# The expert stage of a mixer, cross-attention and mixture-of-experts layer on one core: row gathers recorded two experts ahead, apart from their transposes

## The chip, the core and the metric

The kernel runs on one core of one Trainium2 chip. The core has five engines with an instruction queue each: TensorE (PE; its weight loads are listed apart as PEld), VectorE (DVE), ScalarE (ACT), GpSimd (POOL) and SyncE (SP), which here issues transfers and reads registers. Data moves by 16 DMA engines. The metric is the device time of one execution in microseconds (us), lower is better.

## What is computed

The reference is one layer of a streaming encoder: a mixer of attention and gated linear attention, a cross-attention, and a mixture of experts. The change touches the last. Each of 2048 tokens of 1024 channels goes to two of 32 experts, and an expert is a gated pair of projections to 512 channels and one back:

```python
def _hier_moe(h, norm_g, w_group, b_group, w_expert, b_expert, w_gate, w_up, w_down):
    xf = _rmsnorm(h, norm_g).reshape(t, d)
    ...                                             # g_sel, top_i, gate: group, two experts in it, their weights
    flat_id = (g_sel[:, None] * EXPERTS_PER_GROUP + top_i).reshape(-1).astype(jnp.int32)
    ...                                             # tokens sorted by expert into x_pad
    def expert_block(args):
        xb, e = args
        hid = jax.nn.silu(xb @ w_gate[e]) * (xb @ w_up[e])
        return hid @ w_down[e]
    ...
    out = out_pad[dest] * flat_gate[order][:, None].astype(out_pad.dtype)
    y = jnp.zeros((t, d), out.dtype).at[token_of].add(out)
```

## The kernel before

**Number format.** Values in 32 bits are carried as two 16-bit halves, so each product is three matmuls. The weights of an expert, 6 MB, come in 12 loads of 512 KB (`est`, line 1499, issued by SP, pool E of 8 buffers). Each is split into its halves `ew` by one ACT instruction and then one DVE instruction, into pool W of 28 buffers: the 24 of two experts, and 4 for tokens.

**The order.** All instructions are first recorded. A list scheduler then fixes one order for each engine, from the order of recording and some shifts, by a model of durations. Buffers of a pool open in the order of recording, and an engine works strictly in its order. So a wait at the head of an engine's queue holds all that is behind it.

**The expert stage** (`stage_moe`, line 1444) goes through 32 places, which this text numbers 0 to 31: place 0 holds late tokens of expert 0, place 1 is expert 1, and from place 2 on experts come ranked by their number of tokens (`rank`, line 1372, leaves that order in the tensor `order`). `expert_weights` reads a ranked expert's number into a register of SP (the rows `TENSOR_LOAD order`, line 1478). A place has room for 104 to 224 tokens, in blocks of up to 128. A second part of the 128-row places, as the 32 rows of place 20, is its second block.

**One block** goes through these steps: SP loads its list of row numbers and gates (`lt`, line 1533, 6 buffers); POOL gathers the rows of the normed activations, 4 KB a row in two halves of 16 bits, with an indirect DMA (`ex<-xnS,lt`, line 1536, pool Q of 4 buffers); PE transposes them in 16 pieces (`pxT`, pool mm of 3 PSUM banks, 8 pieces to a bank); ACT copies the first bank and DVE the second to `exT` (pool W). Then `expert` (line 1552) does the gate and up products (`pgu`), `sil` and `hid`, and the down product (`py`, in the same 3 banks). ACT scales the result to `ey`, and POOL adds it to the output with an indirect DMA (`out_dram<-ey`, line 1603, here called the scatter). A list buffer is free when its block's scatter has landed, since that reads it; blocks of 64 rows or fewer copy the row numbers to `dst` for their scatter.

**How far ahead.** In the recording, `prepare(n + 1)` stands in front of `expert(n)`: the list, the gather and the transposes of a place are all recorded one place ahead, behind its weights.

Of the kernel before, what the change touches and what calls it, by code (L numbers as in the profile page):

```python
# [8 lines left out]
F16 = mybir.dt.float16  # L9
# [21 lines left out]
NG, NE, DE = 4, 32, 512  # L31
LIST = S + 256
FRONT = -3000
# [5 lines left out]
THR = 0  # L39
CHAIN = 1  # L40
# [4 lines left out]
STAG = "W"  # L45
FIXED = 2
LATE = 2
# [6 lines left out]
CAPS = [224, 190, 182, 172, 168, 160, 160, 154, 152, 150, 148, 146, 144, 142, 138, 136, 132, 128, 128, 126,  # L54
        124, 122, 118, 118, 116, 114, 112, 112, 106, 104, 160, 176, 32]


TAGS = {"W": (4096, 28), "E": (4096, 8), "P": (4096, 3), "X": (4096, 4), "Q": (4096, 4), "t2": (2048, 4), "t1": (1024, 2), "r": (160, 5), "lt": (32, 6),
        "s8": (32, 5), "sq": (32, 6), "mx": (32, 8), "cb": (32, 6), "so": (32, 6), "c8": (32, 5), "c9": (32, 6), "q8": (32, 4), "grT": (512, 1)}
BANKS = {"mm": 3, "av": 1, "sc": 4}  # L60
AP = bass.AP
# [39 lines left out]
class Program:  # L101
# [15 lines left out]
    def tile(self, pool, shape, dtype, name, tag, bufs):  # L117
        t = pool.tile(shape, dtype, name=name, tag=tag, bufs=bufs)
        self.tags[t.tensor.name] = tag
        self.bufs[tag] = bufs  # L120
        return t
# [266 lines left out]
class Layer:  # L388
# [10 lines left out]
    def tile(self, tag, name, shape, dtype, parts=128):  # L399
        assert parts * 0 + mybir.dt.size(dtype) * math.prod(shape) <= TAGS[tag][0], (name, tag)  # L400
        return self.prog.tile(self.sb, [parts] + shape, dtype, name, tag, TAGS[tag][1])

# [1028 lines left out]
    def begin_moe(self):  # L1431

        nc = self.nc
        self.ident16 = self.gate_b[:, 128:192].bitcast(F16)
        nc.vector.tensor_copy(self.ident16, self.ident)
        which, need, self.first = self.expert_weights(None, 0)
        self.prog.shift = EARLY
        cap = CAPS[NE - FIXED]
        tokens = self.tokens(cap, which, need, blocks=LATE)
        self.second = self.expert_weights(None, 1, [self.last] if THR else [], CHAIN)  # L1440
        self.expert(cap, self.first, tokens)
        self.prog.shift = 0

    def stage_moe(self):

        slots = [NE] + [NE - FIXED + e for e in range(1, FIXED)]
        n = (NE - FIXED) // 3
        slots += [k + j * n for k in range(n) for j in range(3)]
        ready = {}

        def prepare(n):
            s = slots[n]
            if n == 0:
                which, need, w = lambda: NE, (), self.first
            elif n < FIXED:
                which, need, w = self.second
            else:
                if n == FIXED:
                    self.rank()
                which, need, w = self.expert_weights(s, None)  # L1460
            self.prog.shift = FRONT
            ready[n] = w, self.tokens(CAPS[s], which, need)
            self.prog.shift = 0
        prepare(0)
        for n, s in enumerate(slots):
            if n + 1 < len(slots):
                prepare(n + 1)
            self.prog.shift = -3000
            self.expert(CAPS[s], *ready.pop(n))
            self.prog.shift = 0  # L1470

    def expert_weights(self, rank, e, after=(), chain=0):

        nc, a, prog = self.nc, self.a, self.prog
        reg = []
        need = []
        if e is None:
            need = [prog.call("sync", lambda nc: reg.append(nc.sync.value_load(
                self.order[0:1, rank:rank + 1], min_val=0, max_val=NE - 1)), [], [self.order], method="value_load")]
        which = (lambda: reg[0]) if e is None else (lambda: e)  # L1480
        return which, need, self.split_expert(which, need + list(after), STAG if e == 0 else "E", chain)

    def split_expert(self, which, need, tag="E", chain=0):
        self.prog.group = "ew"
# [19 lines left out]
            return lambda half, i: tiles[i // k][:, half, i % k]  # L1504
        return get("w_e_gate", D, DE, 2), get("w_e_up", D, DE, 2), get("w_e_down", DE, D, 1)

    def tokens(self, cap, which, need, first=None, blocks=0):

        self.prog.group = "tk"
        nc, prog = self.nc, self.prog  # L1510
        xT = [self.tile("W", "exT", [8, cap], F16) for _ in range(2)]
        rest = []
        for t0 in range(0, cap, 128):
            n = min(128, cap - t0)
            lt = self.tile("lt", "lt", [2], I32)

            parts = 4 if n <= 32 else 2 if n <= 64 else 1

            g = -(-n // 16) * 16
            m = g if parts == 1 else 128 // parts  # L1520
            rest.append((t0, m, lt, parts))

            def load(nc, lt=lt, m=m, t0=t0, parts=parts):
                e = which()
                if first is not None:
                    src = self.lists[bass.ds(first(), m)]
                elif isinstance(e, int):
                    src = self.lists[e * LIST + t0:e * LIST + t0 + m]
                else:
                    src = self.lists[bass.ds(e * LIST + t0, m)]  # L1530
                if parts > 1:
                    src = src[None].to_broadcast([parts, m, 2])
                return nc.sync.dma_start(lt[:m * parts], src)
            prog.call("sync", load, [lt[:m * parts]], [self.lists], need)
            x = self.tile("Q", "ex", [2, D], F16)
            prog.call("gpsimd", lambda nc, x=x, lt=lt, g=g: nc.gpsimd.indirect_dma_start(
                out=x[:g].rearrange("p t d -> p (t d)"), out_offset=None, in_=self.xnS[:S + OFF - blocks * 128],
                in_offset=bass.IndirectOffsetOnAxis(ap=lt[:g, 0:1], axis=0)), [x[:g]],
                      [lt[:g], self.xnS[:S + OFF - blocks * 128]])
            for h in range(2):  # L1540
                p = self.prog.tile(self.ps, [128, 8, 128], F16, "pxT", "mm", BANKS["mm"])
                for k in range(8):

                    d = slice(k // 2 * 256 + k % 2, (k // 2 + 1) * 256, 2)
                    nc.tensor.transpose(p[:, k, :n], x[:n, h, d], self.ident16[:n, :n])
                if h:
                    nc.vector.tensor_copy(xT[h][:, :, t0:t0 + n], p[:, :, :n])
                else:
                    nc.scalar.copy(out=xT[h][:, :, t0:t0 + n], in_=p[:, :, :n])
        return xT, rest  # L1550

    def expert(self, cap, weights, tokens):
        self.prog.group = "ex"
        nc, prog = self.nc, self.prog
# [53 lines left out]
    def stage_over(self):  # L1608
        nc = self.tc.nc
        self.prog.direct = True  # L1610
        count = self.cp.tile([1, 1], F32, name="count")
        nc.vector.memset(count, 0.0)
        total = nc.values_load(self.total[0:1, 0:1], min_val=0, max_val=64)  # L1613
        with self.tc.For_i(0, total, 1):
            sel = self.tile("r", "sel", [NL], F32, 1)
            t = self.tile("r", "ot", [NL], F32, 1)
            f = self.tile("r", "of", [2], F32, 1)
            at = self.tile("r", "oi", [2], I32, 1)
            before, upto, ids, place = (self.over[:, n] for n in range(4))

            nc.vector.tensor_scalar(sel, before, count, None, op0=OP.is_le)
            nc.vector.tensor_scalar(t, upto, count, None, op0=OP.is_gt)
            nc.vector.tensor_tensor(out=sel, in0=sel, in1=t, op=OP.mult)
            nc.vector.tensor_tensor(out=t, in0=sel, in1=ids, op=OP.mult)
            nc.vector.tensor_reduce(out=f[:, 0:1], in_=t, op=OP.add, axis=AX.X)
            nc.vector.tensor_scalar(t, before, count, -128.0, op0=OP.subtract, op1=OP.mult)
            nc.vector.tensor_tensor(out=t, in0=t, in1=place, op=OP.add)
            nc.vector.tensor_tensor(out=t, in0=sel, in1=t, op=OP.mult)
            nc.vector.tensor_reduce(out=f[:, 1:2], in_=t, op=OP.add, axis=AX.X)
            nc.vector.tensor_copy(at, f)  # L1630
            nc.vector.tensor_scalar(count, count, 1.0, None, op0=OP.add)
            e = nc.sync.value_load(at[0:1, 0:1], min_val=0, max_val=NE - 1)
            row = nc.sync.value_load(at[0:1, 1:2], min_val=0, max_val=NL * LIST - 128)
            which = lambda: e
            w = self.split_expert(which, ())
            self.expert(128, w, self.tokens(128, which, (), lambda: row))


# [24 lines left out]
```

## Time and profile before

| | |
|---|---|
| median of 3 runs | 2382.82 us (2374.73 to 2393.74) |
| profiled execution, device time | 2377.83 us |
| its span, first to last instruction | 2376.1 us |
| mean granted TensorE clock | 0.967 |
| PE busy over the span | 2137.9 us (90%) |
| DVE, ACT, POOL busy | 1559.7 (66%), 1339.2 (56%), 750.6 (32%) us |
| expert weight loads | 384 of 512 KB |

The expert stage begins at about 1660 us of the span and lasts to its end. The page cuts the span into 40 slices of about 59 us. Their lines for PE's busy tenths, the granted clock, the busy tenths of the DMA engines and the traffic are:

```profile
PE   6999999999888889889998999994899999888888
PEclk9999999999989999999999999997899999999999
DMA  9544246663357686888785556495989999999995
GB/s 258 155 114 116 81 142 178 192 191 103 111 116 149 145 179 151 184 169 201 168 211 131 116 143 126 117 250 140 300 303 329 345 369 331 325 338 340 358 346 152
```

The expert stage is the last 12 or so of them, with traffic of 300 to 369 GB/s, but for the last slice, against 81 to 258 before. In a row of the trace, a number in brackets is how long the engine was idle before that row, and the arrow names what ended it.

### The profile page before, as it was taken

To read this page: it belongs to the slowest core of one execution; us is meant where nothing else is said; L and a number is where in the kernel's file an instruction comes from. 1 tells how busy PE (TensorE), PEld (TensorE's weight loads), DVE (VectorE), ACT (ScalarE), POOL (GpSimd) and SP (SyncE) were. 2 spreads that over 40 slices of the span, in tenths; PEclk is the share of its full clock that TensorE was granted. 3 is DMA by queue.
4 is the path that set the end of the run, shared out by engine and by line. 5 is a ranking of instruction groups with operands and counts; after the bars stand their busy time and mean duration, and the time that the engine had idled before them with its cause. 6 is when DMAs were issued, how large, how long until landed. Compare 5 with 4: busy or idle time off the path is not lost. (4 is left out here: it accounts for less than half of the span.)

```text
span 2376.1 us, 55935 instructions
## 1 busy us (share of the span) xinstructions
PE 2137.9 (90%) x22153; PEld 1466.6 (62%) x22153; DVE 1559.7 (66%) x3434; ACT 1339.2 (56%) x2848; POOL 750.6 (32%) x622
## 2 busy tenths in 40 slices
PE   6999999999888889889998999994899999888888
PEld 3456646556444445445665777843777887777666
DVE  7454445655588888888534655476666877777774
ACT  6455345554466666665433333444566777667775
POOL 1444235552134444444221222213132322222111
PEclk9999999999989999999999999997899999999999
DMA  9544246663357686888785556495989999999995
GB/s 258 155 114 116 81 142 178 192 191 103 111 116 149 145 179 151 184 169 201 168 211 131 116 143 126 117 250 140 300 303 329 345 369 331 325 338 340 358 346 152
DMA packets 504232, 485.34 MB, mean 204 GB/s; under 512 B 391364, under 2 KB 401886, under 8 KB 503966
## 3 DMA queue, kind: packets, MB, share of 16 engines
q1 hardware_dynamic: 489950, 442.11, 64.9%
q0 software_dynamic: 14016, 39.63, 7.2%
q8 instruction: 175, 2.87, 0.5%
q14 instruction: 91, 0.75, 0.1%
HBM read 306.28 MB, written 83.61 MB: 164 GB/s over the span
## 5 line engine op out<-in xcount | busy, mean ns | idle before, releaser
L166 DVE SCALAR_TENSOR_TENSOR ew<-est,ew 128x1024 f16<-128x1024 f32 x384 | 459.8, 1220 | 95.1 <-ACT ew L166 91.5
L166 PE MATMUL pgu<-exT,ew 128*128 128x160 f16 (+27 forms) x6336 | 451.5, 227 | 4.8 <-issue 2.3
L166 PEld LDWEIGHTS <-ew 128*128 128x128 f16 x6336 | 409.7, 100 | 13.6 <-issue 7.5
L166 ACT ACTIVATE ew<-est 128x1024 f16<-128x1024 f32 x384 | 392.8, 1051 | 33.7 <-DMA est<-in_w_e_down_dram 23.9
L166 PEld LDWEIGHTS <-uT 128*128 128x128 f16 x1920 | 187.7, 98 | 224.1 <-issue 9.7
L166 PE MATMUL py<-ew,hid 128*128 128x512 f16 (+4 forms) x1584 | 244.8, 348 | 8.2 <-DVE hid L166 6.2
L166 PE MATMUL sc<-KC,qT 128*128 128x512 f16 (+3 forms) x640 | 171.0, 359 | 57.9 <-ACT e L166 53.9
L166 ACT ACTIVATE e<-sc,m 128x512 f32<-128x512 f32 (+3 forms) x288 | 179.2, 631 | 75.6 <-DVE m L166 49.0
L166 POOL TENSOR_TENSOR e<-e 128x1024 f16<-128x1024 f32 (+7 forms) x96 | 152.3, 1591 | 215.5 <-ACT e L166 165.7
L166 DVE TENSOR_REDUCE mx<-sc 128x1 f32<-128x512 f32 (+3 forms) x320 | 185.4, 603 | 51.1 <-PE sc L166 50.8
L166 PE MATMUL ph<-wo,mT 128*128 128x512 f16 x768 | 194.2, 380 | 8.2 <-DMA mT<-mcd 3.9
L166 PE MATMUL pc<-hT,wcq 128*128 128x128 f16 x3072 | 193.8, 220 | 1.6 <-DMA hT<-hcS 1.0
L166 PEld LDWEIGHTS <-wcq 128*128 128x128 f16 x3072 | 181.6, 98 | 4.9 <-DMA hT<-hcS 1.5
L166 PE MATMUL phc<-wco,prT 128*128 128x512 f16 x768 | 175.9, 382 | 4.3 <-DMA prT<-prc 4.3
L166 PEld LDWEIGHTS <-hid 128*128 128x128 f16 (+4 forms) x1584 | 106.0, 104 | 108.9 <-issue 19.9
L1603 POOL DMA_INDIRECT out_dram<-ey,lt x33 | 65.0, 1969 | 263.9 <-ACT ey L166 218.2
L166 PEld LDWEIGHTS <-qT 128*128 128x128 f16 x640 | 60.0, 99 | 118.4 <-issue 75.8
L166 PE MATMUL po<-VC,pT 128*128 128x128 f16 x1632 | 123.1, 221 | 6.2 <-DMA pT<-e 4.9
L166 PEld LDWEIGHTS <-prT 128*128 128x128 f16 x768 | 74.2, 98 | 87.0 <-DMA prT<-prc 4.4
L166 PEld LDWEIGHTS <-mT 128*128 128x128 f16 x768 | 72.6, 98 | 83.2 <-DMA mT<-mcd 5.8
L166 PEld LDWEIGHTS <-pT 128*128 128x128 f16 x1632 | 103.6, 99 | 29.2 <-DMA pT<-e 9.7
L166 ACT CAST e<-e 128x1024 f16<-128x1024 f32 (+7 forms) x96 | 76.5, 798 | 69.1 <-DVE e L166 36.0
(320 smaller groups left out, 3700.1 us busy)
## 6 DMA issues: line engine op xcount, KB each, us to landing
est<-in_w_e_gate_dram SPq DMA_DIRECT2D x128, 512.0 KB
est<-in_w_e_up_dram SPq DMA_DIRECT2D x128, 512.0 KB
est<-in_w_e_down_dram SPq DMA_DIRECT2D x128, 512.0 KB
wst<-in_w_in_dram SPq DMA_DIRECT2D x20, 512.0 KB
xt<-in_x_dram SPq DMA_DIRECT2D x16, 512.0 KB
uS<-uT SPq DMA_DIRECT2D x16, 512.0 KB
ust<-in_w_ckv_dram SPq DMA_DIRECT2D x16, 512.0 KB
uT<-uS SPq DMA_DIRECT2D x16, 512.0 KB
```

The costliest lines, as they stand in the source:

```text
L166: o.fn = fn or (lambda nc: getattr(getattr(nc, eng), method)(*a, **k))
L1603: self.prog.call("gpsimd", lambda nc: nc.gpsimd.indirect_dma_start(out=out, out_offset=bass.IndirectOffsetOnAxis(ap=rows, axis=0), in_=y, ...
```

## The change

`tokens` is split in two. `fetch` records a block's list load and its gather; `turn` records its transposes and copies. `fetch(n + 2)` stands in the recording in front of `prepare(n + 1)` and `expert(n)`, `turn` stays in `prepare`. Reading the expert's number moves with `fetch` into a function of its own (`chosen`), and `rank` is called in `fetch(2)`. The list pool goes from 6 to 12 buffers; pool Q stays at 4. The instructions are the same in kind and number.

```diff
-TAGS = {"W": (4096, 28), "E": (4096, 8), ... "Q": (4096, 4), ... "lt": (32, 6),
+TAGS = {"W": (4096, 28), "E": (4096, 8), ... "Q": (4096, 4), ... "lt": (32, 12),
...
-        def prepare(n):
+        def fetch(n):
             s = slots[n]
             if n == 0:
-                which, need, w = lambda: NE, (), self.first
+                which, need = lambda: NE, ()
             elif n < FIXED:
-                which, need, w = self.second
+                which, need, _ = self.second
             else:
                 if n == FIXED:
                     self.rank()
-                which, need, w = self.expert_weights(s, None)
+                which, need = self.chosen(s)
             self.prog.shift = FRONT
-            ready[n] = w, self.tokens(CAPS[s], which, need)
+            rows[n] = which, need, self.fetch(CAPS[s], which, need)
             self.prog.shift = 0
+
+        def prepare(n):
+            which, need, got = rows.pop(n)
+            w = self.first if n == 0 else self.second[2] if n < FIXED else self.split_expert(which, need)
+            self.prog.shift = FRONT
+            ready[n] = w, self.turn(CAPS[slots[n]], got)
+            self.prog.shift = 0
+        fetch(0)
+        fetch(1)
         prepare(0)
         for n, s in enumerate(slots):
+            if n + 2 < len(slots):
+                fetch(n + 2)
             if n + 1 < len(slots):
                 prepare(n + 1)
```

The scheduler decides where the moved instructions land. Three places show it. The first is **POOL's queue** around the two gathers of place 20 (128 and 32 rows), before. The three scatters ahead of them are of places 16 and 17 (both blocks), the one behind is of place 18.

```order
L1603 DMA out_0_dram<-ey_4121,lt_4059 2176x1024
L1603 DMA out_0_dram<-ey_4167,lt_4104 2176x1024
L1603 DMA out_0_dram<-ey_4170,dst_4172 8704x256
L1536 DMA ex_4245<-xnS_1033,lt_4244 128x2048
L1536 DMA ex_4249<-xnS_1033,lt_4248 32x2048
L1603 DMA out_0_dram<-ey_4212,lt_4150 2176x1024
```

In the changed kernel the same two gathers are `ex_4176` and `ex_4178`. The scatters ahead of them are of place 15; the gather `ex_4129` is place 19's and `ex_4223` place 21's; the scatters behind are of place 16 (`ey_4125`) and place 17 (`ey_4169`).

```order
L1624 DMA out_0_dram<-ey_4076,lt_3942 2176x1024
L1624 DMA out_0_dram<-ey_4079,dst_4081 8704x256
L1546 DMA ex_4129<-xnS_1033,lt_4128 128x2048
L1546 DMA ex_4176<-xnS_1033,lt_4175 128x2048
L1546 DMA ex_4178<-xnS_1033,lt_4177 32x2048
L1624 DMA out_0_dram<-ey_4125,lt_3988 2176x1024
L1546 DMA ex_4223<-xnS_1033,lt_4222 128x2048
L1624 DMA out_0_dram<-ey_4169,lt_4035 2176x1024
```

The gathers of place 20 have moved ahead of three scatters: those of place 16 and of both blocks of place 17. Behind place 16's scatter there is already a gather of place 21.

The second is **SP's queue**, the list of place 20's first block (`lt_4244` before, `lt_4175` after). `est_4173` to `est_4187` before are weights of place 19.

```order
L1499 DMA est_4183<-in_w_e_up_dram 128x1024
L1499 ISA
L1499 DMA est_4185<-in_w_e_up_dram 128x1024
L1533 ISA
L1533 DMA lt_4244<-lists_1034 128x2
L1499 ISA
L1499 DMA est_4187<-in_w_e_up_dram 128x1024
```

After, the weights around it (`est_3996` to `est_4000`) are those of place 15:

```order
L1512 DMA est_3996<-in_w_e_gate_dram 128x1024
L1512 ISA
L1512 DMA est_3998<-in_w_e_up_dram 128x1024
L1543 ISA
L1543 DMA lt_4175<-lists_1034 128x2
L1512 ISA
L1512 DMA est_4000<-in_w_e_up_dram 128x1024
```

The list load stands four places further ahead, as far as six more buffers let it; both wait for the landing of a scatter, of place 16 before and of place 12 after.

The third is **the start of the stage on SP**, the first weights of place 2. Before, its 4 gate loads and 3 of its 4 up loads stand ahead of a block of 20 register reads:

```order
L1533 ISA
L1533 DMA lt<-lists 128x2
L1499 ISA
L1499 DMA est<-in_w_e_gate_dram 128x1024
L1499 ISA
L1499 DMA est<-in_w_e_gate_dram 128x1024
```

After, there are four more lists ahead of the first gate load. This piece is the last three of these lists and three gate loads, and with its last row the register reads begin:

```order
L1543 DMA lt<-lists 128x2
L1543 ISA
L1543 DMA lt<-lists 128x1x2
L1543 ISA
L1543 DMA lt<-lists 128x2
L1512 ISA
L1512 DMA est<-in_w_e_gate_dram 128x1024
L1512 ISA
L1512 DMA est<-in_w_e_gate_dram 128x1024
L1512 ISA
L1512 DMA est<-in_w_e_gate_dram 128x1024
L1487 TENSOR_LOAD order
```

So 26 register reads and 2 more lists now stand between place 2's third and fourth gate loads, and one more read ahead of the first up load; before, the reads stood behind the third up load.

## Rows read from the trace of the kernel before

**Rows 1.** Busy time, granted clock, DMA share and traffic by stretch of the span:
```profile
core 0: us, PE busy (x) PEld busy (x) DVE busy (x) ACT busy (x) POOL busy (x), PEclk, DMA share, GB/s
1713.00:1760.00 47.00, 46.99 (x490) 38.63 (x488) 30.22 (x44) 29.99 (x46) 10.48 (x6) 1.00 0.88 289
1760.00:2320.00 560.00, 510.80 (x6774) 416.10 (x6773) 423.09 (x579) 407.06 (x612) 141.44 (x81) 0.95 1.01 342
1840.00:1960.00 120.00, 120.00 (x1563) 97.87 (x1561) 95.61 (x135) 92.78 (x141) 35.11 (x19) 1.00 1.02 356
```
**Rows 2.** Groups of PE's instructions in 1684 to 2340 us; after the bar, idle time:
```profile
line engine op names shapes xcount | busy us, mean ns | idle before us <-releasers
L166 PE MATMUL pxT<-gb,ex 128*128 128x128 f16 (+25 forms) x736 | 44.9, 203 | 52.7 <-ACT exT L166 27.7 <-DMA ex<-xnS,lt 20.7 <-DVE exT L166 3.3
```
**Rows 3.** PE's waits in 1684 to 2340 us:
```profile
engine line waited for: us in total, times, longest us
PE pxT L166 <- ACT exT L166: 27.7, 6, 7.6
PE pxT L166 <- DMA ex<-xnS,lt: 20.7, 7, 4.8
```
**Rows 4.** Timeline of POOL, place 20's two gathers:
```profile
start us, us, engine line op out<-in xcount [idle before <-releaser]
2086.66 1.00 POOL L1536 DMA_INDIRECT ex<-xnS,lt  x1 [0.30 <-issue]
2087.97 1.50 POOL L1536 DMA_INDIRECT ex<-xnS,lt  x1 [0.30 <-issue]
```
**Rows 5.** Timeline of PE: transposes in 2022 to 2058 us, then place 20's:
```profile
2044.08 0.37 PE L166 MATMUL pxT<-gb,ex 32*128 32x32 f16 x8 [4.58 <-ACT exT L166]
...
2050.29 0.61 PE L166 MATMUL pxT<-gb,ex 128*128 128x128 f16 x8
...
2095.54 1.24 PE L166 MATMUL pxT<-gb,ex 128*128 128x128 f16 x16 [3.32 <-DMA ex<-xnS,lt]
```
**Rows 6.** DMA issues in 1684 to 2340 us, median us from issue to landing:
```profile
ex<-xnS,lt POOLq DMA_INDIRECT x46, 9.2
```
**Rows 7.** POOL's waits in 1684 to 2340 us:
```profile
POOL ex L1536 <- DMA lt<-lists: 58.0, 10, 15.5
```
**Rows 8.** The waits of SP's queue in 1684 to 2340 us:
```profile
SPq L1533 <- DMA out_dram<-ey,lt: 35.4, 13, 6.0
SPq L1533 <- ACT ey L166: 9.9, 8, 2.4
```
**Rows 9.** Stretches behind three of the seven waits; columns as in Rows 1:
```profile
1833.50:1840.30 6.80, 4.68 (x50) 4.61 (x51) 0.84 (x1) 1.06 (x1) 0.97 (x1) 0.50 1.04 330
2028.00:2031.40 3.40, 3.40 (x39) 3.40 (x37) 0.71 (x1) 0.00 (x0) 0.00 (x0) 0.50 1.07 306
2096.30:2099.70 3.40, 3.40 (x39) 3.40 (x37) 1.00 (x1) 0.00 (x0) 0.00 (x0) 0.50 1.07 316
```
**Rows 10.** Timeline of ACT, the copy that ends a wait for a bank:
```profile
2043.04 1.26 ACT L166 COPY exT<-pxT 128x1024 f16<-128x1024 f16 x2
```
**Rows 11.** Timeline of SP's queue at the start of the stage:
```profile
1658.13 2.10 SPq L1499 DMA_DIRECT2D est<-in_w_e_gate_dram  x4
1660.46 13.93 SPq L1499 DMA_DIRECT2D est<-in_w_e_up_dram  x4
...
1682.27 1.57 SPq L1499 DMA_DIRECT2D est<-in_w_e_down_dram  x3
```
**Rows 12.** Timeline of ACT in place 1, splits of place 2's weights:
```profile
1681.17 3.89 ACT L166 ACTIVATE ew<-est 128x1024 f16<-128x1024 f32 x4
...
1690.27 1.06 ACT L166 ACTIVATE ew<-est 128x1024 f16<-128x1024 f32 x1 [0.16 <-DMA est<-in_w_e_down_dram]
1696.87 0.32 ACT L166 ACTIVATE sil<-pgu 128x176 f32<-128x176 f32 x1 [5.55 <-PE pgu L166]
```
**Rows 13.** Timeline of PE in place 1:
```profile
1694.05 0.82 PE L166 MATMUL pxT<-gb,ex 96*128 96x96 f16 x8 [4.78 <-DMA ex<-xnS,lt]
```

More of the change, by code (lines that the diff above doesn't have):

```diff
@@ L55 @@
         124, 122, 118, 118, 116, 114, 112, 112, 106, 104, 160, 176, 32]
-TAGS = {"W": (4096, 28), "E": (4096, 8), "P": (4096, 3), "X": (4096, 4), "Q": (4096, 4), "t2": (2048, 4), "t1": (1024, 2), "r": (160, 5), "lt": (32, 6),
+TAGS = {"W": (4096, 28), "E": (4096, 8), "P": (4096, 3), "X": (4096, 4), "Q": (4096, 4), "t2": (2048, 4), "t1": (1024, 2), "r": (160, 5), "lt": (32, 12),
         "s8": (32, 5), "sq": (32, 6), "mx": (32, 8), "cb": (32, 6), "so": (32, 6), "c8": (32, 5), "c9": (32, 6), "q8": (32, 4), "grT": (512, 1)}
@@ L1435, in begin_moe @@
         nc.vector.tensor_copy(self.ident16, self.ident)
-        which, need, self.first = self.expert_weights(None, 0)
+        which, need, self.first = self.expert_weights(0)
         self.prog.shift = EARLY
         cap = CAPS[NE - FIXED]
-        tokens = self.tokens(cap, which, need, blocks=LATE)
-        self.second = self.expert_weights(None, 1, [self.last] if THR else [], CHAIN)
+        tokens = self.turn(cap, self.fetch(cap, which, need, blocks=LATE))
+        self.second = self.expert_weights(1, [self.last] if THR else [], CHAIN)
         self.expert(cap, self.first, tokens)
@@ L1448, in stage_moe @@
         slots += [k + j * n for k in range(n) for j in range(3)]
-        ready = {}
-        def prepare(n):
+        ready, rows = {}, {}
+        def fetch(n):
             s = slots[n]
             if n == 0:
-                which, need, w = lambda: NE, (), self.first
+                which, need = lambda: NE, ()
             elif n < FIXED:
-                which, need, w = self.second
+                which, need, _ = self.second
             else:
@@ L1470, in stage_moe, with chosen, expert_weights @@
             self.prog.shift = 0
-    def expert_weights(self, rank, e, after=(), chain=0):
-        nc, a, prog = self.nc, self.a, self.prog
+    def chosen(self, rank):
         reg = []
[L1476 to L1481, printed above, removed]
+        need = [self.prog.call("sync", lambda nc: reg.append(nc.sync.value_load(
+            self.order[0:1, rank:rank + 1], min_val=0, max_val=NE - 1)), [], [self.order], method="value_load")]
+        return (lambda: reg[0]), need
+    def expert_weights(self, e, after=(), chain=0):
+        which = lambda: e
+        return which, [], self.split_expert(which, list(after), STAG if e == 0 else "E", chain)
     def split_expert(self, which, need, tag="E", chain=0):
@@ L1505, in split_expert, with fetch @@
         return get("w_e_gate", D, DE, 2), get("w_e_up", D, DE, 2), get("w_e_down", DE, D, 1)
-    def tokens(self, cap, which, need, first=None, blocks=0):
+    def fetch(self, cap, which, need, first=None, blocks=0):
         self.prog.group = "tk"
         nc, prog = self.nc, self.prog
-        xT = [self.tile("W", "exT", [8, cap], F16) for _ in range(2)]
-        rest = []
+        rows = []
         for t0 in range(0, cap, 128):
@@ L1520, in tokens @@
             m = g if parts == 1 else 128 // parts
-            rest.append((t0, m, lt, parts))
             def load(nc, lt=lt, m=m, t0=t0, parts=parts):
@@ L1539, in tokens, with turn @@
                       [lt[:g], self.xnS[:S + OFF - blocks * 128]])
+            rows.append((t0, n, x, m, lt, parts))
+        return rows
+    def turn(self, cap, rows):
+        self.prog.group = "tk"
+        nc = self.nc
+        xT = [self.tile("W", "exT", [8, cap], F16) for _ in range(2)]
+        rest = []
+        for t0, n, x, m, lt, parts in rows:
+            rest.append((t0, m, lt, parts))
             for h in range(2):
@@ L1635, in stage_over @@
             w = self.split_expert(which, ())
-            self.expert(128, w, self.tokens(128, which, (), lambda: row))
+            self.expert(128, w, self.turn(128, self.fetch(128, which, (), lambda: row)))
 def kernel(**inputs):
```

## The prediction

> **What bounds the kernel now.** The change touches only the expert stage, so I read that alone, first the table by stretch. From 1760 to 2320 us PE is busy 510.8 of 560 us [rows 1], the DMA engines are occupied all the time (share 1.01), and DVE and ACT are busy three quarters of it. PE is nearest to its limit, and what it loses should show as idle time. The view of groups says where: nearly all of PE's idle time stands ahead of the transposes, 52.7 us [rows 2]. The view of waits splits it [rows 3]: 20.7 us in seven waits are for the gathered rows, 27.7 us in six are for ACT's copy that gives a PSUM bank back. Only the first kind is what the change is about. The timeline of place 20 shows one [rows 4, 5]: the gather starts on POOL at 2086.66, PE goes on at 2095.54, 8.9 us later, after 3.32 us of idling; a gather takes 9.2 us to land in the median [rows 6]. POOL issued it at once when its queue came to it (0.30, issue), so it was late because of what stood in front of it, scatters of places 16 and 17. Ten other gathers waited on POOL for their list, 58.0 us in all [rows 7].
>
> A second stretch tells what the memory side could do. From 1840 to 1960 us PE is busy 120.00 of 120 us at full clock, with 356 GB/s; over the 560 us it is 342 [rows 1].
>
> **The change part by part.** *Gathers earlier.* In POOL's new order place 20's gathers stand behind the scatters of place 15. What they need then is a list and a free buffer of pool Q. The list stands four places further ahead on SP. The buffers come from the transposes four gathers earlier, of places 17 and 18, which are done by 2044.45 and 2050.90 [rows 5]; the first gather could go about 48 us before PE wants it at 2092.2 (2095.54 less 3.32), the second behind it 41 us, against a landing of 9.2. The other late gathers move by one or two places in the same way. So I expect the seven waits to go: 20.7 us, of which 4.78 is in place 1 [rows 13], which I take apart, and 15.9 in six later ones.
>
> *What follows the waits.* Behind three of these later waits PE ran at a granted clock of 0.50, the lower of its two levels, for 6.80, 3.40 and 3.40 us [rows 9]; each followed an idle PE, and in the undisturbed 120 us no such stretch stands (clock 1.00) [rows 1]. With a PE that doesn't idle, half of this comes back, 13.6 / 2 = 6.8 us. Also, some waits for a bank come a few us behind a gather wait: in place 18 PE stood 4.58 us [rows 5] until ACT copied at 2043.04 [rows 10], late because the same ACT had run dry and then had splits of weights queued. Those may go with the cause, or stay, since ACT's order does not change: between 0 and 27.7 us. I put them at 0.
>
> *The limit on the way back.* The bytes are the same. 560 us at 342 GB/s are 191.5 MB; at the 356 GB/s of the undisturbed stretch they take 538 us. Up to 22 us can be won there if that is the pace the transfers keep. The terms, 15.9 + 6.8 = 22.7, reach this limit, so I take 22. The lower end is the waits alone, 15.9.
>
> The Trainium skill ("Perfetto Trace Analysis", section Identifying the Most-Contended Engine) says to judge DMA by the utilization of memory, since the occupancy of 16 DMA engines misleads. The trace agrees: the share is 1.02 at 356 GB/s and 1.01 at 342. By the share there would be nothing to win, by the rule the same 22 us as above.
>
> *The start of the stage.* Here the change costs. Before, place 2's gate loads went out in 2.10 us from 1658.13 and three up loads behind 1660.46, and only then 20 register reads held SP; the four up loads with the reads between them took 13.93 us [rows 11], so a read is at most 0.70 us. Now 26 reads, and 6 lists at about the 0.5 us of a load's issue, come ahead of the fourth gate load: 26 x 0.70 + 6 x 0.5 = 21 us, so it goes out at about 1681 instead of 1660, and the third up load at about 1683.5. A load issued from 1682.27 on landed at 1690.27, where ACT waited for it [rows 11, 12], at most 8 us later. So these four land by about 1691, and ACT, which split them from 1681.17 to 1685.06 [rows 12], does so some 7 us later. Behind them in ACT's order stand the `sil` of place 1, for which PE's banks and then the down product wait. What covers it: ACT idled 5.55 us for PE in this place [rows 12], and PE no longer stands 4.78 us for its gather. The gain of 4.78 is used up; I take 0, between 4.8 gained and 7 - 5.55 = 1.5 lost. The transfers that are put off there are caught up later, at 289 GB/s from 1713 to 1760 [rows 1] there is room under 356.
>
> *Lists and scatters.* Twelve list buffers cost no time. A scatter can now stand on POOL behind a gather that waits for its Q buffer, as place 17's behind the gather of place 21. That one needs a buffer whose transposes are place 18's, near 2050 us [rows 5], while place 17's scatters went out shortly before 2086.66 [rows 4]. I take 0; the price if that is wrong is a rival below.
>
> **The sum**: 22 + 0 = 22 us off the profiled execution of 2377.83 gives 2355.8. The median of the runs is 2382.82, 5.0 above that execution, so in the median's terms it is **2360.8 us**. Own range of this case: 15.9 less 1.5 is 14.4 us, 2368; 22 + 4.8 is 26.8 us, 2356.
>
> **The rivals.** *The weights set the pace.* If loading and splitting are the real limit, PE arrives earlier at a place and waits for `ew`, or the bank waits grow by what the gather waits give up, since ACT's copies stand behind its splits. For it: the DMA share of 1.01, and 27.7 us of bank waits already. Against it: PE was fully busy for 120 us at 356 GB/s. Between nothing and a fourth of the 22 us comes back: 2377 to 2384.
>
> *The gathers are still late*, that is, the change does not do what it says. For it: gathers wait for lists now, and lists for scatters (35.4 and 9.9 us on SP) [rows 8]. Against it: the lists stand four places ahead. Time about 2383, and I count it with the case above.
>
> *All of it goes.* If the bank waits are a consequence of the gather waits, 52.7 [rows 2] + 6.8 come back, 59.5 us: 2323. Against it: this needs 191.5 MB in about 505 us, 379 GB/s, above the 356 of the undisturbed stretch.
>
> *Slower: lists hold the weights.* SP waits at a list for the landing of a scatter, 45.3 us in 21 waits, 6.0 the longest [rows 8], and all weight loads stand behind it. If a scatter is held on POOL by a gather in front that waits for its Q buffer, its list buffer comes later, and the weights with it. Eight weight buffers, 4.2 MB at 356 GB/s, cover 11.8 us; with the 2.2 us of a mean wait now, a hold of over 9.6 us more decides. At as many waits as now, 2 us each beyond the cover use up the gain and 20 us more (21 x 2 = 42, less 22): 2403. Against it stand the times just given: the buffer is free some 35 us before place 17's scatters go.
>
> **How the numbers follow.** Forecast 0.62, the weights' pace or late gathers 0.20, all of it 0.08, slower 0.10. The forecast stands near the bound of 1%, which is 23.8 us (2359.0) and about what a measurement of this kernel can tell from no change. I give it a good half on the far side, because the bank waits that I put at 0 can only add: 0.35 of its 0.62. Faster by over 1%: 0.35 + 0.08 = 0.43. Within 1%: 0.27 + 0.20 = 0.47. Slower: 0.10. The range leaves out the last two rivals, 0.18 together: from 2342, half way from the forecast to the case in which all of it goes ((2360.8 + 2323) / 2), to 2385, the end of the weights' pace.
>
> **What would show it.** Right: waits of the transposes for the gathers near 0, POOL's gathers no longer waiting for lists, gathers issued over 9.2 us ahead everywhere, about 356 GB/s and a clock near 1.00 from 1760 us on, and the third up load of place 2 at about 1683.5 us without PE ending place 1 later. The weights' pace: waits for the bank grow over 27.7 us, or PE waits for `ew`, with traffic still at 342. Slower: the list waits on SP far over 45 us, and ACT waiting for loads. The forecast is wrong if the gathers are on time and the idle time of PE is still about 50 us.

## The result and the profile after

The changed kernel takes 2349.09 us in the median (2346.08 to 2356.16, 4 runs) against 2380.76 us before (4 runs): a ratio of 0.9864, 95% interval 0.9816 to 0.9912. Beside the experiments it was run again: 2356.42 us against 2385.12, ratio 0.9881, interval 0.9864 to 0.9899. So the change wins 1.2 to 1.4%, 29 to 32 us; forecast were 22 us, 2360.8, with an own range of 14.4 to 26.8 us.

First the stretches, as in [rows 1], of the changed kernel:

```profile
core 0: us, PE busy (x) PEld busy (x) DVE busy (x) ACT busy (x) POOL busy (x), PEclk, DMA share, GB/s
1713.00:1760.00 47.00, 47.00 (x508) 39.23 (x508) 32.54 (x45) 32.87 (x47) 11.14 (x7) 1.00 1.00 332
1760.00:2320.00 560.00, 531.39 (x7190) 433.90 (x7188) 450.30 (x613) 431.86 (x651) 126.54 (x81) 0.98 1.02 353
1840.00:1960.00 120.00, 118.61 (x1540) 96.34 (x1538) 95.22 (x131) 91.83 (x139) 32.47 (x21) 1.00 1.03 356
```

In the same 560 us PE is busy 20.6 us more, that is, it gets further. PE's waits in 1684 to 2314 us answer to [rows 3]; the two largest kinds that are left:

```profile
engine line waited for: us in total, times, longest us
PE pxT L166 <- ACT exT L166: 20.5, 5, 5.8
PE pxT L166 <- DVE exT L166: 5.3, 2, 3.3
```

No wait of a transpose for a gather is left, out of seven with 20.7 us; of the 27.7 us of waits for ACT's copy of a bank 20.5 are still there. POOL in 1684 to 2314 us, against [rows 7]:

```profile
POOL ex L1546 <- PE pxT L166: 132.7, 23, 12.8
```

No gather waits for a list. Most of their waiting is for a buffer of pool Q, that is, they go as soon as there is room. Place 20's two gathers, against [rows 4, 5]:

```profile
2031.77 1.28 POOL L1546 DMA_INDIRECT ex<-xnS,lt  x1 [2.98 <-PE pxT L166]
2036.34 0.87 POOL L1546 DMA_INDIRECT ex<-xnS,lt  x1 [3.29 <-PE pxT L166]
...
2077.34 1.07 PE L166 MATMUL pxT<-gb,ex 128*128 128x128 f16 x16
```

The first stands 45.6 us ahead of its transposes, where it stood 8.9.

The span of one execution also holds how late the stage began, which differs by some us from run to run. So I compare a fixed piece of work, from PE's first product of place 2 to its first of place 30, the times read from the timeline of PE. It is 1713.3 to 2334.4 before and 1716.7 to 2308.6 after:

```profile
1716.70:2308.60 591.90, 563.29 (x7451) 459.50 (x7449) 470.82 (x641) 452.99 (x678) 133.05 (x86) 0.98 1.02 356
1716.70:2032.70 316.00, 308.71 (x3969) 252.21 (x3967) 248.44 (x344) 239.48 (x361) 77.22 (x50) 0.99 1.02 352
2032.70:2308.60 275.90, 254.58 (x3483) 207.29 (x3482) 222.38 (x297) 213.50 (x319) 55.84 (x37) 0.96 1.02 360
```

```profile
1713.30:2334.40 621.10, 571.89 (x7451) 465.57 (x7449) 465.10 (x639) 448.24 (x673) 152.98 (x88) 0.96 1.00 338
1713.30:2047.80 334.50, 316.55 (x3972) 258.46 (x3970) 247.38 (x344) 237.93 (x358) 94.77 (x51) 0.97 0.99 335
2047.80:2334.40 286.60, 255.34 (x3481) 207.12 (x3480) 217.72 (x295) 210.31 (x315) 58.22 (x38) 0.95 1.01 342
```

The upper fence is the changed kernel, the lower the kernel before; the rows are places 2 to 29, 2 to 16 and 17 to 29. The piece is 29.2 us shorter: PE idles 28.6 instead of 49.2 us, 20.6 less, and is busy 8.6 us less for the same instructions, at a granted clock of 0.98 instead of 0.96.

### The profile page after: what moved, and what is told of

It reads as the page before. It is cut to its first block, busy times and chain, and to the rows that moved or that the text cites. A ratio compares the mean times of both kernels' runs of the same rounds, so it can differ in the third digit from the quotient of the medians.

```text
span 2350.0 us, 55929 instructions
## 1 busy us (share of the span) xinstructions
PE 2135.1 (91%) x22153; PEld 1463.1 (62%) x22153; DVE 1558.2 (66%) x3434; ACT 1339.7 (57%) x2848; POOL 736.1 (31%) x622
## 4 chain that ended last, share of the span: by engine, by line
PE 37%; DMA 4%; issue 3%; ACT 3%; DVE 2%; SPq 1%; POOL 1%; another core or an unknown queue 0%; POOLq 0%; ACTq 0%; DVEq 0%
PE pgu L166 14%; PE py L166 8%; PE pc L166 5%; PE phc L166 4%; PE pcs L166 2%; PE pxT L166 2%; ACT ew L166 1%; DMA lists<-row,dest 1%; PE ph L166 1%; DVE ew L166 1%; SPq L1487 1%; DMA xTr<-xc 1%; DMA est<-in_w_e_up_dram 1%; SPq L166 0%; POOL rqc L166 0%
## 5 line engine op out<-in xcount | busy, mean ns | idle before, releaser
L166 PEld LDWEIGHTS <-ew 128*128 128x128 f16 x6336 | 404.7, 98 | 15.1 <-issue 9.2
L1624 POOL DMA_INDIRECT out_dram<-ey,lt x33 | 56.5, 1712 | 234.5 <-ACT ey L166 197.4
L166 PEld LDWEIGHTS <-pT 128*128 128x128 f16 x1632 | 105.2, 100 | 28.3 <-DMA pT<-e 7.1
L1546 POOL DMA_INDIRECT ex<-xnS,lt x52 | 67.7, 1302 | 161.0 <-PE pxT L166 133.0
```

Source lines behind the costliest of these rows:

```text
L166: o.fn = fn or (lambda nc: getattr(getattr(nc, eng), method)(*a, **k))
L1624: self.prog.call("gpsimd", lambda nc: nc.gpsimd.indirect_dma_start(out=out, out_offset=bass.IndirectOffsetOnAxis(ap=rows, axis=0), in_=y, ...
```

## The experiments

Twelve runs were made, of eleven kernels. Ratios are to the kernel before on the same chip. "Places 2 to 29" is the piece above.

| kernel | median us | ratio, 95% interval | places 2 to 29, us | PE idle in it |
|---|---|---|---|---|
| changed, again | 2356.42 | 0.9881 (0.9864 to 0.9899) | 590.6 | 26.4 |
| 12 lists only | 2358.86 | 0.9888 (0.9870 to 0.9907) | 597.5 | 31.3 |
| 8 lists only | 2355.42 | 0.9900 (0.9878 to 0.9923) | 601.0 | 35.0 |
| two ahead, 6 lists | 2381.63 | 0.9988 (0.9968 to 1.0008) | 624.1 | 55.1 |
| changed, spare bank | 2373.76 | 0.9962 (0.9940 to 0.9984) | 589.5 | 25.1 |
| changed, half the weight bytes | 2342.87 | 0.9850 (0.9827 to 0.9873) | 587.9 | 26.0 |
| changed, no up loads | 2359.68 | 0.9894 (0.9846 to 0.9942) | 596.5 | 29.6 |
| changed, reads priced | 2348.75 | 0.9848 (0.9818 to 0.9879) | 593.6 | 27.8 |
| changed, reads priced, again | 2345.03 | 0.9856 (0.9834 to 0.9878) | 593.9 | 28.3 |
| 12 lists only, reads priced | 2357.38 | 0.9907 (0.9883 to 0.9931) | 597.0 | 33.2 |

Two more, no low halves (0.9883) and no third product (0.9803), stand below. The piece and PE's idling are read from one profile of each run; between two profiles of the same kernel they differ by up to 1.3 and 2.2 us.

### Which part of the change frees the gathers: lists or recording

The change has two parts, so each was run alone. The kernel before with 12 list buffers:

```diff
-"lt": (32, 6),
+"lt": (32, 12),
```

> The kernel before with 12 list buffers instead of 6 and nothing else of the change; the gathers are still recorded one place ahead. In POOL's order its gathers nevertheless stand one to two places earlier, almost as in the changed kernel. Theory A, the lists held the gathers: the time is that of the changed kernel, 2349 us within 6, a ratio of 0.986 to the kernel before, and no wait of a transpose for its gather is left after 1760 us. Theory B, the recording two places ahead is what frees them: 2365 to 2381, with some of the seven gather waits (20.7 us) still there.

Theory A holds by the ratio, 0.9888, and by the waits; the time of 2358.86 lies 4 us above its range, as the changed kernel beside it, 2356.42, lies 1 us above. No transpose waits for a gather, and POOL's gathers wait for Q buffers instead of lists, as in the changed kernel (POOL in 1684 to 2340 us):

```profile
POOL ex L1536 <- PE pxT L166: 131.3, 25, 13.0
```

The gathers of this kernel are still recorded one place ahead, behind the weights. In POOL's queue they stand early all the same, since the list scheduler puts a gather as soon as its model has the list there and a buffer free. Its place 20, on POOL:

```profile
2026.62 1.95 POOL L1536 DMA_INDIRECT ex<-xnS,lt  x1 [0.30 <-issue]
...
2039.45 0.99 POOL L1536 DMA_INDIRECT ex<-xnS,lt  x1 [2.32 <-DMA est<-in_w_e_gate_dram]
2046.43 1.04 POOL L1536 DMA_INDIRECT ex<-xnS,lt  x1 [5.98 <-PE pxT L166]
```

The last two rows are place 20's gathers, the first is that of place 19. They stand 47 and 41 us ahead of their transposes.

The other half, the changed kernel with 6 list buffers:

```diff
-"lt": (32, 12),
+"lt": (32, 6),
```

> The changed kernel with the 6 list buffers of before: the gathers are recorded two places ahead, but POOL's order is nearly that of the kernel before. Theory A (lists): the time of before, 2381 within 8, with gather waits of about 20 us and gathers that wait for lists about 58 us. Theory B (recording): 2349 within 6.

The time is that of before (0.9988). Gathers wait for lists, and transposes for gathers, as before; the rows are of POOL and of PE in 1684 to 2340 us:

```profile
POOL ex L1546 <- DMA lt<-lists: 84.8, 14, 20.1
...
PE pxT L166 <- DMA ex<-xnS,lt: 26.7, 8, 7.7
```

So the recording two places ahead, which the change is named after, gives nothing without the lists. A list buffer is busy from its load to the landing of its block's scatter, and six of them reach back three to four places. The changed kernel itself, in the same group:

> The changed kernel itself, beside the others on one chip. Both theories: ratio 0.986, 2349 us within 6; it is what the other kernels of this group are compared with.

It came out at 0.9881, in its interval the same as 12 lists alone. Eight buffers, one third of the addition, do nearly as well:

```diff
-"lt": (32, 6),
+"lt": (32, 8),
```

> The kernel before with 8 list buffers instead of 6, nothing else. In POOL's order a gather stands about one place further ahead than before, half of what 12 buffers give. Theory A, lists hold the gathers and 9.2 us ahead are enough: the gather waits go and the time is that of 12 buffers, a ratio of 0.987 to 0.991. If two places ahead are needed: 0.993 to 1.0.

The ratio is 0.9900 and no transpose waits for a gather, though six gathers on POOL still wait for lists (POOL in 1684 to 2314 us):

```profile
POOL ex L1536 <- DMA lt<-lists: 52.5, 6, 18.0
```

It takes only so much lead that a gather lands before PE wants it. But the ratio flatters this kernel: its places 2 to 29 take 601.0 us, 20 less than before and 9 more than in the changed kernel. Ahead of them, from PE's first product of the stage to the first of place 2, it takes 72.0 us, 6 less than the changed kernel; the cause of that stays open.

Does the recording add anything beside the lists? In places 2 to 29 the changed kernel needs 591.9 and 590.6 us in its two profiles, 12 lists alone 597.5. A second pair tells the same, below (593.6 and 593.9 against 597.0). These are 3 to 7 us, all of them in places 2 to 16, from one profile or two of each kernel. The spans of whole executions tell it in one pair (0.9856 against 0.9907, intervals that do not meet) and not in the other (0.9881 against 0.9888).

### What limits the changed kernel: transfers, banks, splits or PE

The prediction held that the way back ends at the traffic of 356 GB/s. This experiment leaves half the bytes of each weight load out and keeps every instruction of every engine in its place; the splits read the half that was loaded twice, so the weights are other ones:

```diff
-return nc.sync.dma_start(st, s[:, r:r + k * 128].rearrange("e (p k) f -> p (e k) f", p=128))
+part = s[:, r:r + k * 128].rearrange("e (p k) f -> p (e k) f", p=128)
+return nc.sync.dma_start(st[:, :1, :512], part[:, :1, :512])
...
-self.halves(t[:, 0], t[:, 1], st, WS)
+half = st[:, 0, None, :512].to_broadcast([128, 2, 512])
+self.halves(*(t[:, n].rearrange("p k (a c) -> p (k a) c", c=512) for n in range(2)), half, WS)
```

> The changed kernel with every instruction in the same place on every engine, but each weight load brings only half of its bytes (256 KB), and the splits read that half twice: some 94 MB of traffic are left out. Theory D, transfers set the pace of the changed kernel in the short places: the 20 us of waits for a bank and nearly all other idling of PE after place 2 go, and PE at full clock is left, 2315 to 2325. Rival, ACT's and DVE's splits set it: the waits for a bank stay, 2345 to 2356.

The rival was right about the waits, and the time is 2 us under its range. The rows are places 2 to 29 and then PE's waits of this kernel (1684 to 2314 us):

```profile
1707.90:2295.80 587.90, 561.88 (x7451) 458.78 (x7449) 471.18 (x641) 451.71 (x680) 133.97 (x86) 0.98 0.77 208
...
PE pxT L166 <- ACT exT L166: 19.8, 4, 5.3
```

Traffic is 208 instead of 356 GB/s, and places 2 to 29 take 587.9 us instead of 591.9 and 590.6; the waits for a bank are the same. So half of the weight bytes costs the changed kernel 3 to 4 us there. Its own trace agrees: in places 2 to 29 ACT waits for weight loads in five waits, 2.1 us in all. In the whole time it stands at 0.9850 against 0.9864 and 0.9881 of the changed kernel.

What PE waits for is seen in place 19 of this same kernel. PE, and behind it ACT:

```profile
2066.51 1.36 PE L166 MATMUL pxT<-gb,ex 128*128 128x128 f16 x24
2067.80 9.86 PE L166 MATMUL pgu<-exT,ew 128*128 128x114 f16 x192
2082.79 0.37 PE L166 MATMUL pxT<-gb,ex 32*128 32x32 f16 x8 [5.12 <-ACT exT L166]
```

```profile
2067.08 2.95 ACT L166 ACTIVATE ew<-est 128x1024 f16<-128x1024 f32 x3
...
2076.93 0.29 ACT L166 CAST hid<-sil 128x114 f16<-128x114 f32 x1 [1.32 <-DVE sil L166]
2077.12 1.05 ACT L166 ACTIVATE ew<-est 128x1024 f16<-128x1024 f32 x1
2078.08 0.25 ACT L166 ACTIVATE sil<-pgu 128x114 f32<-128x114 f32 x1
2079.65 0.29 ACT L166 CAST hid<-sil 128x114 f16<-128x114 f32 x1 [1.32 <-DVE sil L166]
2079.84 2.00 ACT L166 ACTIVATE ew<-est 128x1024 f16<-128x1024 f32 x2
2081.75 0.99 ACT L166 COPY exT<-pxT 128x1024 f16<-128x1024 f16 x1
```

24 of place 20's 32 transposes, which fill the three banks, are done by about 2067.9, but ACT's copy that frees the first bank for the last eight comes at 2081.75. In ACT's order it stands behind nine splits of the next place's weights and the four `sil` and `hid` of place 19, and the `hid` wait for DVE, whose own splits stand in front of them. Place 19 is short, 9.86 us of products, and PE reaches the end of them first. No load is waited for: ACT has no wait for a weight load from 1684 to 2314 us. The same copy has PE waiting in the kernel before (upper row) and in the changed kernel:

```profile
2112.63 0.35 PE L166 MATMUL pxT<-gb,ex 32*128 32x32 f16 x8 [4.33 <-ACT exT L166]
...
2094.20 0.36 PE L166 MATMUL pxT<-gb,ex 32*128 32x32 f16 x8 [5.13 <-ACT exT L166]
```

One experiment changes this order by the way. Without the loads of the up weights (the gate's buffer is split twice) the scheduler has fewer loads to place:

```diff
-loads = []
+loads, kept = [], {}
...
-st = self.tile(tag, "est", [k, cols], F32)
+st = self.tile(tag, "est", [k, cols], F32) if name != "w_e_up" else kept[r]
+kept[r] = st
...
-loads.append(prog.call("sync", load, [st], [], ...))
+if name != "w_e_up":
+    loads.append(prog.call("sync", load, [st], [], ...))
```

> The changed kernel without the loads of the up weights: the gate weights' buffers are split a second time in their place, so a third of the weight traffic, about 63 MB, is left out, and the work of PE, ACT and DVE is the same. Theory D, transfers set the pace of the changed kernel: PE is busy 505 of 534 us, so the 29 us of idling and what the lower clock costs come back, 2310 to 2325. Rival, PE and ACT set it: 2345 to 2352.

Neither expectation holds: 0.9894 in two runs, no gain over the changed kernel. PE and ACT of this kernel at place 19:

```profile
2113.50 0.36 PE L166 MATMUL pxT<-gb,ex 32*128 32x32 f16 x8
...
2112.14 1.30 ACT L166 COPY exT<-pxT 128x1024 f16<-128x1024 f16 x2
```

Here the copies stand behind four splits and one `sil`, and the transposes wait for nothing. The two halves of its piece are:

```profile
1719.60:2061.20 341.60, 319.47 (x3967) 254.07 (x3964) 243.06 (x342) 234.57 (x356) 86.42 (x49) 0.96 0.77 235
2061.20:2316.10 254.90, 247.45 (x3487) 202.09 (x3486) 219.30 (x301) 209.45 (x322) 91.30 (x38) 0.99 0.88 279
```

Places 17 to 29 take 254.9 us, 21.0 less than in the changed kernel. Places 2 to 16 take 341.6, 25.6 more, with new waits of the down product for `hid`, 22.2 us. The work of PE, ACT and DVE is the same. Together with the half loads, which left the order alone, this points to the order on ACT and DVE as what sets the rest of PE's idling. That another order would also do with all the bytes was not tried, so it is not shown; nor was less work for ACT.

The bank itself was tried too, with the first of a block's two transposed halves in a PSUM bank that the stage does not use:

```diff
-p = self.prog.tile(self.ps, [128, 8, 128], F16, "pxT", "mm", BANKS["mm"])
+tag = "mm" if h else "av"
+p = self.prog.tile(self.ps, [128, 8, 128], F16, "pxT", tag, BANKS[tag])
```

> The changed kernel, with the first of a block's two transposed halves in the PSUM bank that the stage leaves unused, so that transposes no longer share their three banks with the down product for that half. Theory C, the 20.5 us of waits for a bank are a matter of too few banks: they go, 2329 to 2340. Theory D, PE waits there because it has run ahead of ACT's splits and of the loads (357 GB/s): the wait moves to the products, same time as the changed kernel within 5.

Theory C falls: places 2 to 29 take 589.5 us. The waits for the bank go from 20.5 to 14.1 us in 14 small ones, and in these places 8.6 us of waits appear ahead of the down products, where there were 1.5. The whole is slower (0.9962) by its start alone, 103.7 us from PE's first product of the stage to place 2 instead of 78.4: there POOL's first gathers come to stand behind the scatters of expert 0, and PE waits for one of them (PE's waits in 1634 to 1740 us):

```profile
PE pxT L166 <- DMA ex<-xnS,lt: 20.0, 1, 20.0
```

Less work for DVE and for PE were the last two of this group. In the first, the up weights have no low half (the high half stands for it):

```diff
-self.halves(t[:, 0], t[:, 1], st, WS)
+if name == "w_e_up":
+    nc.scalar.activation(t[:, 0], st, AF.Copy, scale=WS)
+else:
+    self.halves(t[:, 0], t[:, 1], st, WS)
...
-return lambda half, i: tiles[i // k][:, half, i % k]
+return lambda half, i: tiles[i // k][:, 0 if name == "w_e_up" else half, i % k]
```

> The changed kernel without DVE's split of the up weights (the high half stands for the low half too): 128 DVE instructions of 1.22 us less, 156 us. Theory E, DVE's and ACT's splits set the pace in the short places: the waits for a bank go, 2325 to 2335. Theory D, transfers set it: 2345 to 2352.

The ratio is 0.9883 (0.9833 to 0.9933), 2357.05 us in two runs, above the ranges of both theories. In places 2 to 29 DVE is busy 345.0 instead of 470.8 us, yet they take 596.2 us, and the waits for a bank stay (PE in 1684 to 2314 us):

```profile
PE pxT L166 <- ACT exT L166: 19.0, 4, 5.5
PE pxT L166 <- DVE exT L166: 9.2, 3, 3.2
```

So it is not the amount of DVE's work that is waited for. The scheduler changed ACT's order here too, so this run alone does not tell more. In the second, the gate and up products have two matmuls instead of three:

```diff
-nc.tensor.matmul(p[:, j, :cap], w(0, k)[:, c], xT[1][:, k], start=False, stop=False)
```

> The changed kernel without one of the three matmuls of the gate and up products (the one with the second half of the tokens): about 136 us less PE work in the stage. Theory D, transfers set the pace: at most from 357 to some 380 GB/s, so 2315 to 2345, and PE idles over 100 us more. Rival, PE sets it: 2215 to 2260.

It takes 2337.89 us, 0.9803 (0.9755 to 0.9851), in two runs. That is theory D's number, but not for its reason only. In places 2 to 29 PE is busy 475.0 instead of 563.3 us, and they are only 11.5 us shorter (580.4). The waits for a bank grow to 90.4 us in 16, PE idles 96.4 us ahead of the transposes, and ACT waits for loads 23 us in all. What PE no longer does ends in ACT's queue. This does not tell ACT's order from the transfers; for the changed kernel the half loads do.

### The start of the stage

The block of register reads on SP was thinned by giving a read 650 ns in the scheduler's model, where it had 100:

```diff
 if m == "value_load":
-    return 100
+    return 650
```

> The changed kernel, with a register read priced at 650 ns instead of 100 ns in the scheduler's model, near the 0.70 us of the trace: at the start of the stage 7 reads instead of 26 stand ahead of place 2's fourth gate load, and the later order changes little. If the block of reads costs what the prediction feared, 2 to 5 us are won: 2344 to 2347. If it is covered: 2349 within 3.

> The changed kernel with register reads priced near their duration, again, beside the next kernel. If the start of the stage gains by it: ratio 0.983 to 0.987. If the first comparison was chance: 0.988, as the changed kernel.

The ratios are 0.9848 and 0.9856. The two expectations do not agree on them: 2348.75 us is the first one's "covered", 0.9856 the second one's gain. From PE's first product of the stage to the first of place 2 it takes 76.5 and 74.5 us, the changed kernel 78.4 and 79.2, before 79.3 (times from PE's timeline). By this the reads cost the changed kernel some 2 to 5 us, where two profiles of one kernel differ by up to 2. It is the fastest kernel that keeps all the work, but its intervals meet those of the changed kernel. The same with lists alone:

> The kernel before with 12 list buffers and register reads priced near their duration, gathers recorded one place ahead. Theory A (the recording two places ahead gives nothing beside the lists): the time of the kernel ahead of it in this group, within 4 us. Theory B': the recording gives the 2 us by which the changed kernel stood below the one with lists alone, or more.

At 0.9907 it is 12 us slower than its neighbour; theory B' is nearer. Of the 12 us the traces show 3.1 in places 2 to 29 (597.0 against 593.9) and 2.2 in the start (76.7 against 74.5). The two profiled executions differ by only 3.6 us in all (2352.62 and 2349.03), so the traces cannot show where the rest lies; it stays open.

## Why the prediction was right, and where its steps were not

The time lies in the stated range, 2342 to 2385, and the mechanism, late gathers, is the right one. But the gain of 29 to 32 us is above the 22 that were forecast and above the 26.8 that end the prediction's own range of this case; that the stated range holds it is due to the room left for the rival "all of it goes". A gain of over 1% had a chance of 0.43 there, one within 1% had 0.47.

**The seven waits go: right.** None is left, 20.7 us, and from place 3 on every gather stands 28 us or more ahead of its transposes. But the step bundled two things. It took POOL's new order from the whole change, named the list as one thing that a gather needs, and counted the buffers as a cost only ("Twelve list buffers cost no time"). The runs show that the buffers are the cause and the recording is not: 0.9888 with the lists alone, 0.9988 with the recording alone. The row for it was at hand: 58.0 us of gathers waiting for lists [rows 7].

**What follows the waits: right in kind, small in size.** The half-clock stretches were put at 6.8 us; PE's busy time in places 2 to 29 falls by 8.6. The 6.8 count 2.1 us in which PE still idled, since it is busy in only 4.68 of the 6.80 us of the first stretch [rows 9]; half of the busy time is 5.7. The rest came from stretches that the prediction did not count: in these places there are ten with a granted clock of 0.50 before, in which PE is busy 39.6 us, and five after, with 22.8, and half of the difference is 8.4 us. Waits for a bank and other idling were put at 0 of up to 27.7; the idling falls by 20.6, of which the six waits are 15.9, so 4.7 came from there. These two terms, 1.8 and 4.7 us, are what the sum lacked: 22.7 + 6.5 = 29.2, the piece's gain.

**The limit on the way back: wrong.** I held that the gain ends at 356 GB/s, and cut 22.7 to 22. After the change the traffic is 356 GB/s, which looked like a proof. With half the bytes and the same order the piece is only 3 to 4 us shorter. The number agreed because the same bytes were moved in the time that PE and ACT needed; it was a result, not a limit. That the error was cheap, 0.7 us, was luck: the terms in front of it had been put too small and hardly reached the limit. The rule on DMA in the Trainium skill ("Perfetto Trace Analysis", section Identifying the Most-Contended Engine) says which number to read, the utilization of memory rather than occupancy. The half loads show that here neither a share of 1.02 nor 356 GB/s meant that transfers held PE: half of the weight bytes were worth 3 to 4 us.

**The start: right in size, by another path.** In the changed kernel, place 2's loads on SP answer to [rows 11]:

```profile
1665.32 1.51 SPq L1512 DMA_DIRECT2D est<-in_w_e_gate_dram  x3
...
1685.47 0.01 SPq L1512 DMA_DIRECT2D est<-in_w_e_gate_dram  x1
1686.24 2.07 SPq L1512 DMA_DIRECT2D est<-in_w_e_up_dram  x4
```

The fourth gate load goes out 20.2 us after the first, forecast were 23. PE's wait of 4.78 us for a gather is gone, and from the stage's first product to place 2 it takes 78.4 us, 79.3 before, so the term 0 held within 1 us. But the price did not come through the gate loads and ACT's splits: from 1655 to 1717 us ACT has no wait for a load. It came through a list that SP issues behind the reads. DVE waits for it, and PE for the copy that stands behind on DVE, 5.0 us in place 1 (DVE, then PE):

```profile
1687.62 0.21 DVE L166 TENSOR_SCALAR dst<-lt,part 128x1 int32<-128x1 int32 x1 [9.06 <-DMA lt<-lists]
...
1688.85 4.43 PE L166 MATMUL pgu<-exT,ew 128*128 128x176 f16 x39 [4.96 <-DVE exT L166]
```

PE's waits for `hid` there grow from 6.3 to 10.5 us. That the gain and this price are alike was luck.

**The sum.** 29.2 us in places 2 to 29 and 0.9 us ahead are 30 us, as the medians differ (by 31.7 and 28.7). The profiled spans differ by less, 26.1 us, since in the profile after the stage began 4.3 us later (1638.3 against 1634.0).

**The rivals.** "The weights set the pace" and "the gathers are still late" fell. "All of it goes" fell for another reason than given: the waits for a bank are not a consequence of the gather waits, four of the five longest stand at the same short places with or without them, 19, 22, 25 and 28. (The one of 4.58 us in [rows 5] is in place 16, not 18 as the prediction has it; it is the one that went, with 2.0 us for DVE's copy left in its place.) "Lists hold the weights": place 21's gather needs the buffer of place 18's second block, not its first, whose last transposes start at 2066.24 in the profile before, so the margin was 20 us and not 35. And gathers now do wait on POOL in front of scatters, 132.7 us, but the list waits on SP fell, to 19.3 us in 10 and 7.3 us in 9, from the 45.3 of [rows 8].

## What to carry to other kernels

When a transfer is late, ask what its issue waited for and follow that chain to the buffer that comes free last; here a small list, held until a later scatter had landed, kept a 512 KB gather back, and two more list buffers of 1 KB did more than recording the gather earlier. Run each half of a two-part change alone before a cause is named. And a traffic that equals the best stretch is no proof of a limit: halve the bytes with every instruction in its place and see whether the waits go.

## What the runs showed of the hardware that was not expected

A register read on SP took as long as the issue of a load, about 0.6 us. Between the third gate load and the next list stand 17 reads, whose starts in the changed kernel's trace go from 1666.88 to 1676.57, 0.61 us apart in the mean; the first three gate loads start at 1665.32, 1665.92 and 1666.50. The scheduler's model gave a read 0.1 us. And 126 us less DVE work in places 2 to 29, or 42% less traffic (208 against 356 GB/s), each left PE's waits for ACT's copy of a bank nearly as they were, 19.0 and 19.8 us against 20.5.
